# Two of eight convolved channel blocks of a hybrid SSD and conformer layer: their tap products are added by accumulating DMAs instead of by GpSimd

## The chip, the cores and the metric

The kernel runs on one core of a Trainium2 chip. The metric is the device time of that core in microseconds (us). The core's engines have their own instruction queues and wait for each other by semaphores: TensorE (PE in the profile, with PEld for its weight loads), VectorE (DVE), ScalarE (ACT), GpSimd (POOL) and SyncE (SP, which here only issues DMAs). Each queue is worked off in its order: an instruction that waits holds up all that stand behind it.

## The reference, cut to what matters

One layer, 1024 tokens by 1024 channels, all in float32. What is normalized by the first LayerNorm goes through one input projection, whose columns feed an SSD group (Mamba-2, with a convolution of 4 taps) and a conformer group; both meet in an output projection, followed by two more norms and a gate. The conformer group is where the change lies:

```
glu = glu + b_glu[i]
u = glu[..., :D_CONF] * jax.nn.sigmoid(glu[..., D_CONF:])
u = causal_depthwise_conv(u, conf_conv_w[i], conf_conv_b[i])   # 31 taps, 1024 channels
u = jax.nn.silu(layer_norm(u, conf_ln_g[i], conf_ln_b[i]))
y_conf = u * jax.nn.silu(cgate)
```

The convolution is depthwise: each channel's output is a sum of 31 shifted copies of its row, each times one weight. The LayerNorm after it needs all 1024 channels of a token.

## The kernel before, in words

Channels lie on the 128 partitions and the 1024 tokens along the free dimension. The input projection (`inproj`, L188) is made in 44 column tiles of 128 columns. For each, `weights` (L182) has SP load `wraw` (512 KB), ScalarE round it into `wh` and GpSimd take the rest into `wl` (`split`, L117 to L120). TensorE then multiplies for two halves of 512 tokens, for 8 blocks of the contracted dimension, three products each (L123 to L125): 48 matmuls of 128x512 for a column tile. ScalarE takes each half out of PSUM; three banks (`bank`, L77) hold the halves. The tiles `wraw`, `wh` and `wl` rotate through 8 buffers, so `wl` is made ahead of TensorE by two column tiles at most.

The conformer's 1024 channels are 8 blocks. `conf_tile(j)` (L254) makes two column tiles of the projection, then the gated product `u` with 30 columns of padding in front, then the convolution. For six blocks VectorE does all 31 taps into a PSUM tile `pc` (L291). For blocks 1 and 5 (`POOL_CONV`, L36), ScalarE makes the first tap into `acc` (L282) and then, for each of 30 taps, a product `prod` (L285), which GpSimd adds to `acc` (L286). `prod` has two buffers (tag `xd`): the product after next can start when an addition has read its own. Of the sums `acc`, `cs` adds up all eight on GpSimd (L628, L630), and `conf_norm` (L387) needs `cs` complete. Between the conformer's blocks the program places the column tiles of the SSD group: `xbc_tile` (its 4 taps on VectorE, L377) and `z_tile`.

The order of each engine's queue is set when the program is built, by a scheduler that runs the program against estimated durations; it interleaves the products, the casts and the evacuations on ScalarE, and the additions and the `wl` subtractions on GpSimd. After the projection come the normalization, chunks of the SSD scan and the output projections, which the change does not touch.

Of the kernel before, what the change touches and what calls it, by code (L numbers as in the profile page):

```python
# [11 lines left out]
ALU = mybir.AluOpType  # L12
PSUM = bass.MemoryType.PSUM

P = 128
# [10 lines left out]

# columns of the per-channel vectors
VEC = {}
# [18 lines left out]
def tile_block(ctx: ExitStack, tc: tile.TileContext, x, pT, wple, win, wdt, wout, wgate, vec, rows, heads, out):  # L47
# [17 lines left out]

# [1 line left out]
    BUFS = {"gt": 4, "xd": 2, "u": 2, "ha": 3, "y": 2, "xb": 2, "st": 1}  # L67
# [19 lines left out]

# [1 line left out]
    vc = const.tile([P, NVEC], F32, name="vc")  # L89
# [13 lines left out]
    nc.gpsimd.memset(mhalf, -0.5)  # L103
    # [s, l]: 1 where l >= s
    tri = const.tile([P, P], F32, name="tri")
    nc.gpsimd.affine_select(out=tri, in_=ones, pattern=[[1, P]], compare_op=ALU.is_ge, fill=0.0, base=0, channel_multiplier=-1)
    # adds rows h, 16 + h and 32 + h
    fold = const.tile([P, HEADS], F32, name="fold")
# [8 lines left out]
    def split(src, h, l, leng):  # L117
        """h: src rounded to the tensor engine's 12 bits; l: what is left, exactly."""
        nc.scalar.copy(out=h.bitcast(F32R), in_=src)  # L119
        leng.tensor_tensor(out=l.bitcast(F32R), in0=src, in1=h, op=ALU.subtract)  # L120
# [16 lines left out]
    def moments(src, tag):  # L137
        """mean and rstd of the rows of src [P, 1024]."""
        st = wk.tile([P, 2, 6], F32, name="st" + tag, tag="st" + tag)
        for i in range(2):  # L140
            nc.vector.bn_stats(out=st[:, i, :], in_=src[:, i * 512:(i + 1) * 512])
        mv = small("mv" + tag, 2)
        nc.vector.bn_aggr(out=mv, in_=st)
        return mv[:, 0:1], rstd_of(mv[:, 1:2], 1, tag, nc.gpsimd)
# [6 lines left out]

# [1 line left out]
    xts = [regB.tile([P, D], F32, name="xt", tag="B1") for t in range(NT)]  # L153
# [26 lines left out]

# [1 line left out]
    def weights(ct):  # L182
# [17 lines left out]
    def residual():  # L200
        ag, abb, bob = (work(n, "ha") for n in ("ag", "abb", "bob"))
        for i, tl in enumerate((ag, abb, bob)):
            nc.sync.dma_start(out=tl, in_=rows[i:i + 1, :].broadcast_to([P, D]))
        nc.gpsimd.tensor_scalar(out=ag, in0=ag, scalar1=ALPHA, scalar2=0.0, op0=ALU.mult, op1=ALU.add)
        nc.gpsimd.tensor_scalar(out=abb, in0=abb, scalar1=ALPHA, scalar2=0.0, op0=ALU.mult, op1=ALU.add)
        nc.gpsimd.tensor_tensor(out=abb, in0=abb, in1=bob, op=ALU.add)
        # alpha * h + b_out, by tokens
        for t in range(NT):
            nc.gpsimd.tensor_tensor(out=xts[t], in0=xts[t], in1=ag, op=ALU.mult)
            nc.gpsimd.tensor_tensor(out=xts[t], in0=xts[t], in1=abb, op=ALU.add)  # L210
            nc.sync.dma_start(out=ha_d[t], in_=xts[t])

    def ple_all():
        """the projected per-layer input, by tokens."""
        parts = {}
        tags = iter(["u", "u", "xd", "xd", "gt", "gt", "ha", "ha"])
        for src, nm in ((wple, "wp"), (pT, "pp")):
            for k in range(2):
                raw = work(nm + "raw", "xb") if nm == "wp" else regB.tile([P, L], F32, name=nm + "raw", tag="B2")
                parts[nm, k] = (raw, work(nm + "H", next(tags)), work(nm + "L", next(tags)))  # L220
        for half in range(2):
            hs = slice(half * 512, half * 512 + 512)
            for k in range(2):
                for src, nm in ((wple, "wp"), (pT, "pp")):
                    nc.sync.dma_start(out=parts[nm, k][0][:, hs], in_=src[:, k, hs])
                    split(*(a[:, hs] for a in parts[nm, k]), nc.vector)
        embed_load(0)
        nc.sync.dma_start(out=vc, in_=vec)
        nc.vector.tensor_scalar(out=hb, in0=v("bglu", 0, 16), scalar1=0.5, scalar2=None, op0=ALU.mult)
        parts = {i: (a[1].bitcast(F32R), a[2].bitcast(F32R)) for i, a in parts.items()}  # L230
        for t in range(NT):
            tk = slice(t * P, (t + 1) * P)
            pl = work("pl", "xb" if t % 4 > 1 else "y", L)
            for n in range(2):
                nn = slice(n * 512, n * 512 + 512)
                ps = bank("psp")
                for k in range(2):
                    three(ps, parts["pp", k][0][:, tk], parts["pp", k][1][:, tk], parts["wp", k][0][:, nn], parts["wp", k][1][:, nn], k == 0, k == 1)
                if (t + n) % 2:
                    nc.vector.tensor_copy(out=pl[:, nn], in_=ps)  # L240
                else:
                    nc.scalar.copy(out=pl[:, nn], in_=ps)
            nc.sync.dma_start(out=ple_d[t], in_=pl)
# [10 lines left out]
    def conf_tile(j):  # L254
        """GLU and the causal convolution of 128 channels."""
        ga = work("ga", "gt")
# [24 lines left out]
        if j in POOL_CONV:  # L281
            nc.scalar.activation(out=acc, in_=u[:, 0:L], func=AF.Identity, scale=v("ccw", j * KC), bias=v("ccb", j))  # L282
            for i in range(1, KC):
                pr = work("prod", "xd")
                nc.scalar.activation(out=pr, in_=u[:, i:i + L], func=AF.Copy, scale=v("ccw", j * KC + i))  # L285
                nc.gpsimd.tensor_tensor(out=acc, in0=acc, in1=pr, op=ALU.add)  # L286
        else:
            pc = pair("pc")
            first_tap(FT31, pc, u[:, 0:L], v("ccw", j * KC), v("ccb", j))
            for i in range(1, KC):  # L290
                nc.vector.scalar_tensor_tensor(out=pc if i + 1 < KC else acc, in0=u[:, i:i + L], scalar=v("ccw", j * KC + i), in1=pc, op0=ALU.mult, op1=ALU.add)  # L291
# [9 lines left out]
    def dt_path():  # L301
# [7 lines left out]
        nc.sync.dma_start(out=hd, in_=heads.unsqueeze(0).broadcast_to([P, 2, HEADS]))  # L309
        # both parts of the weights side by side  # L310
        nc.scalar.copy(out=wh2[:, :, 0:HEADS].bitcast(F32R), in_=raw)
# [22 lines left out]

        # softplus(v) = max(v, 0) + 2 atanh(e / (2 + e)), e = exp(-|v|)
        nc.vector.tensor_tensor(out=b3(vv), in0=b3(pst[:, 0:P]), in1=bh(hd[:, 0, :]), op=ALU.add)
# [16 lines left out]
    def decays():  # L353
        """dec holds dt * a at first: its sums over the tokens of each chunk, and what follows from them."""
        ar, er = (wk.tile([P, P], F32, name=n, tag="dg") for n in ("ar", "er"))
# [60 lines left out]
    def out_weight(src, get, tag, last, scale=None, leng=nc.gpsimd):  # L416
        """last: a place for the raw one, where those that share the tag leave none."""
        raw = work("wor", last) if last else get("wor", tag)
# [8 lines left out]

# [1 line left out]
    state = work("state", "st")  # L429
# [8 lines left out]
    def prep(c):  # L438
        """what chunk c needs besides the state: decays times C.B, x * dt, B by tokens."""
        xb = slabs(work("xb", "xb", 12 * P), 12)  # L440
# [8 lines left out]
        for q in range(2):  # L449
            er = ea_d[c * HEADS:(c + 1) * HEADS, :].rearrange("(t q) l -> q t l", q=2)[q]  # L450
            nc.sync.dma_start(out=ea[q * HD:(q + 1) * HD], in_=er.unsqueeze(0).broadcast_to([HD, NK, P]))
        # exp(acs[l] - acs[s]); the part l < s is held at exp(0) here and dropped with C.B
        for h in range(HEADS):
# [30 lines left out]
    def chunk(c, sz, xb, gg, ea, xdt, xdd, btok):  # L484
        y = slabs(work("y", "y"))
        for g in range(2):
            # from the state, scaled by exp(acs[l])
            ys = y[:, g * 4:g * 4 + 4, :]
# [34 lines left out]
    def mean_square(c, y, ea):  # L523
        """rstd of the two groups of channels of the gated output."""
        sq = ea.rearrange("p (g t) l -> p g t l", g=2)
# [21 lines left out]
    def conf_out(c, mH, mL, ha):  # L547
        """conformer half of the output projection"""
        for n in range(2):
# [14 lines left out]
    def affine(o, src, mu, rs, g, b):  # L564
        """(src - mu) * rs * g + b"""
        nc.vector.scalar_tensor_tensor(out=o, in0=src, scalar=mu, in1=g, op0=ALU.subtract, op1=ALU.mult)
        nc.vector.scalar_tensor_tensor(out=o, in0=o, scalar=rs, in1=b, op0=ALU.mult, op1=ALU.add)

    def out_proj(c, yH, yL):
        """the SSM half of the output projection, and the norm"""  # L570
        r = work("r", "ha")
# [21 lines left out]
    def gate(c, r, hTH, hTL):  # L593
        """the per-layer input, gated, and the norm"""
        pl = work("pl3", "st")
# [75 lines left out]

# [1 line left out]
    ready, last = out_proj(0, *ys.pop(0)), None  # L673
# [58 lines left out]
```

## Time and profile before

| | |
|---|---|
| runs of the kernel | 928.87 and 934.99 us, median 931.93 |
| profiled execution, span from the first to the last instruction | 927.1 us |
| the lower of the two runs less that span | 1.8 us |
| busy: PE, DVE, POOL, ACT | 877.1, 708.6, 534.4, 364.8 us |
| busy share of POOL from 150 to 250 us and from 350 to 450 us | 0.94 to 0.98 |
| the 60 additions into `acc` on GpSimd | 160.2 us |

An engine's busy time counts its compute instructions; matmuls overlap, so that the busy time of PE is no measure of how fast it works, while the distance between the starts of two matmuls is. Where an engine stands idle, the profile names what released it. The share of busy time is of the whole span; the change lies in two stretches of it.

### The profile page before, as it was taken

The numbers are of one execution on the slowest core, as the hardware profiler recorded it, in microseconds if no ns is written. First come the engines' busy times: TensorE is split into PE (matmuls) and PEld (weight loads), VectorE is DVE, ScalarE is ACT, GpSimd is POOL, SyncE is SP. The second block draws the span as 40 slices with busy tenths as digits, with TensorE's granted clock in tenths as the row PEclk, the third lists the DMA queues.
The fourth block names the chain that finished last, engine by engine and source line by source line (L and its number), as shares of the span: only waits on it lengthen the run. The fifth ranks groups of instructions, "written<-read, shape, count | busy, mean of one in ns | idle before, by whom it ended". The sixth has DMA issues, their size and how long they took to land.

```text
span 927.1 us, 10959 instructions
## 1 busy us (share of the span) xinstructions
PE 877.1 (95%) x4141; PEld 711.0 (77%) x4141; DVE 708.6 (76%) x830; ACT 364.8 (39%) x513; POOL 534.4 (58%) x298
## 2 busy tenths in 40 slices
PE   6989998989999999999899999999999889999996
PEld 5857787868787888788688887777777668888885
DVE  7868997498999989989626523998885786666665
ACT  3532244665423435555446533644343421111001
POOL 2559836999924249999792254676757442222211
PEclk9999999989999999999999999999999999999999
DMA  9703241321213121322322388888887902222111
GB/s 337 264 24 107 77 157 46 96 69 46 78 37 113 52 86 53 123 97 80 114 100 83 103 304 271 300 273 230 283 264 261 353 25 92 91 90 91 69 46 68
DMA packets 67716, 126.42 MB, mean 136 GB/s; under 512 B 4176, under 2 KB 41552, under 8 KB 67664
## 3 DMA queue, kind: packets, MB, share of 16 engines
q1 hardware_dynamic: 67664, 125.73, 40.4%
q8 instruction: 32, 0.52, 0.2%
q14 instruction: 20, 0.16, 0.1%
HBM read 89.93 MB, written 35.78 MB: 136 GB/s over the span
## 4 chain that ended last, share of the span: by engine, by line
PE 47%; DVE 20%; POOL 13%; DMA 11%; issue 6%; ACT 3%; SPq 1%; POOLq 0%; DVEq 0%; ACTq 0%
POOL acc L286 8%; DVE pc L291 7%; PE ps L123 6%; PE ps L124 6%; PE ps L125 6%; DVE cacc L377 4%; PE psg L123 3%; PE psg L125 3%; PE psg L124 3%; DMA wor<-in_wout_dram 3%; PE pss L123 3%; PE pss L125 3%; PE pss L124 3%; DMA xb<-xbc_d 2%; POOL wl L120 2%
## 5 line engine op out<-in xcount | busy, mean ns | idle before, releaser
L123 PE MATMUL ps<-hH,wl 128*128 128x512 f32 x704 | 278.4, 397 | 12.7 <-ACT ga L262 6.2
L124 PE MATMUL ps<-hL,wh 128*128 128x512 f32 x704 | 278.0, 395 | 1.0 <-DVE hL L179 1.0
L125 PE MATMUL ps<-hH,wh 128*128 128x512 f32 x704 | 278.1, 395 | 0.0
L291 DVE SCALAR_TENSOR_TENSOR pc<-u,vc,pc 128x1024 f32<-128x1024 f32 x174 | 223.8, 1286 | 4.5
L123 PEld LDWEIGHTS ps<-hH,wl 128*128 128x128 f32 x704 | 133.9, 191 | 44.7 <-issue 7.7
L286 POOL TENSOR_TENSOR acc<-acc,prod 128x1024 f32<-128x1024 f32 x60 | 160.2, 2671 | 13.3 <-ACT acc L282 9.3
L124 PEld LDWEIGHTS ps<-hL,wh 128*128 128x128 f32 x704 | 134.2, 191 | 29.3 <-DVE hL L179 1.5
L125 PEld LDWEIGHTS ps<-hH,wh 128*128 128x128 f32 x704 | 134.2, 191 | 28.4 <-issue 0.2
L120 POOL TENSOR_TENSOR wl<-wraw,wh 128x1024 fp32r<-128x1024 f32 x44 | 110.6, 2513 | 53.2 <-ACT wh L119 23.0
L132 POOL TENSOR_SCALAR ve<-mv 128x1 f32<-128x1 f32 x24 | 21.7, 907 | 121.3 <-DVE mv L611 88.4
L285 ACT ACTIVATE prod<-u,vc 128x1024 f32<-128x1024 f32 x60 | 68.8, 1150 | 51.4 <-POOL acc L286 44.9
L377 DVE SCALAR_TENSOR_TENSOR cacc<-xin,vc,cacc 128x1024 f32<-128x1024 f32 x36 | 76.9, 2135 | 7.4 <-ACT cacc L247 4.7
L119 ACT CAST wh<-wraw 128x1024 fp32r<-128x1024 f32 x44 | 46.2, 1051 | 82.6 <-DMA wraw<-in_win_dram 47.8
L455 DVE TENSOR_SCALAR gt<-gt,acs 128x128 f32<-128x128 f32 x128 | 42.0, 397 | 25.4 <-POOL qs L398 17.3
L123 PE MATMUL psg<-woh,hTL 128*128 128x512 f32 (+1 forms) x136 | 52.9, 389 | 4.8 <-DVE hTL L120 4.8
L123 PE MATMUL pso<-woh,mL 128*128 128x512 f32 x128 | 51.6, 406 | 2.8 <-POOL mL L120 1.8
L123 PE MATMUL pss<-woh,yL 128*128 128x512 f32 x128 | 50.8, 397 | 3.4 <-DVE r L580 3.4
L120 POOL TENSOR_TENSOR wol<-wor,woh 128x1024 fp32r<-128x1024 f32 x12 | 32.7, 2743 | 36.1 <-ACT woh L119 36.1
L125 PE MATMUL pso<-woh,mH 128*128 128x512 f32 x128 | 53.2, 417 | 0.0
L125 PE MATMUL psg<-woh,hTH 128*128 128x512 f32 (+1 forms) x136 | 52.6, 387 | 0.0
L124 PE MATMUL psg<-wol,hTH 128*128 128x512 f32 (+1 forms) x136 | 52.1, 383 | 0.0
L124 PE MATMUL pso<-wol,mH 128*128 128x512 f32 x128 | 50.9, 397 | 0.0
(184 smaller groups left out, 1435.5 us busy)
## 6 DMA issues: line engine op xcount, KB each, us to landing
wraw<-in_win_dram SPq DMA_DIRECT2D x44, 512.0 KB, 4.1
gt<-acs_d SPq DMA_DIRECT2D x16, 512.0 KB, 4.6
wor<-in_wout_dram SPq DMA_DIRECT2D x16, 512.0 KB, 6.1
xbc_d<-cacc SPq DMA_DIRECT2D x12, 512.0 KB, 3.4
xb<-xbc_d SPq DMA_DIRECT2D x8, 768.0 KB, 6.3
xt<-in_x_dram SPq DMA_DIRECT2D x8, 512.0 KB, 9.2
ple_d<-pl SPq DMA_DIRECT2D x8, 512.0 KB, 5.0
ha_d<-xt SPq DMA_DIRECT2D x8, 512.0 KB, 5.2
```

The source lines that it names most:

```text
L119: nc.scalar.copy(out=h.bitcast(F32R), in_=src)
L120: leng.tensor_tensor(out=l.bitcast(F32R), in0=src, in1=h, op=ALU.subtract)
L123: mm(ps, lhsT=ll, rhs=rh, start=first, stop=False)
L124: mm(ps, lhsT=lh, rhs=rl, start=False, stop=False)
L125: mm(ps, lhsT=lh, rhs=rh, start=False, stop=last)
L132: eng.tensor_scalar(out=ve, in0=var, scalar1=EPS, scalar2=None, op0=ALU.add)
L285: nc.scalar.activation(out=pr, in_=u[:, i:i + L], func=AF.Copy, scale=v("ccw", j * KC + i))
L286: nc.gpsimd.tensor_tensor(out=acc, in0=acc, in1=pr, op=ALU.add)
L291: nc.vector.scalar_tensor_tensor(out=pc if i + 1 < KC else acc, in0=u[:, i:i + L], scalar=v("ccw", j * KC + i), in1=pc, op0=ALU.mult, op1= ...
L377: nc.vector.scalar_tensor_tensor(out=acc, in0=xin[:, j:j + L], scalar=v("scw", i * 4 + j), in1=acc, op0=ALU.mult, op1=ALU.add)
L455: nc.vector.tensor_scalar(out=sl, in0=sl, scalar1=col(acs, c, h), scalar2=0.0, op0=ALU.subtract, op1=ALU.min)
```

## The change

The addition of each product to `acc` in blocks 1 and 5 is no longer an instruction of GpSimd's own datapath. GpSimd's queue issues a DMA from `prod` to `acc` (both in SBUF, 128 rows of 4 KB), which adds to what it finds in `acc`. All else in the text of the program stays (the rest of the diff deletes comments, line by line):

```
@@ -283,7 +283,7 @@
             for i in range(1, KC):
                 pr = work("prod", "xd")
                 nc.scalar.activation(out=pr, in_=u[:, i:i + L], func=AF.Copy, scale=v("ccw", j * KC + i))
-                nc.gpsimd.tensor_tensor(out=acc, in0=acc, in1=pr, op=ALU.add)
+                nc.gpsimd.dma_start(out=acc, in_=pr, accum_op=ALU.add)
         else:
             pc = pair("pc")
             first_tap(FT31, pc, u[:, 0:L], v("ccw", j * KC), v("ccb", j))
```

The scheduler orders the queues anew. GpSimd's queue within block 1, before (`x3` stands for three in a row; a name in brackets is a semaphore that is waited for: `DMAHW` of a DMA that SP issued, `DMASW` of one that GpSimd issued, the others of an engine):

```order
L120 TENSOR_TENSOR wl<-wraw,wh 128x1024 [waits DMAHW2_49,PE_49]
L286 TENSOR_TENSOR acc<-acc,prod 128x1024 [waits Activation_49,Pool_49] x3
L120 TENSOR_TENSOR wl<-wraw,wh 128x1024 [waits DMAHW4_49,PE_49]
L286 TENSOR_TENSOR acc<-acc,prod 128x1024 [waits Activation_49,Pool_49] x4
L120 TENSOR_TENSOR wl<-wraw,wh 128x1024 [waits DMAHW5_49,PE_49]
L286 TENSOR_TENSOR acc<-acc,prod 128x1024 [waits Activation_49,Pool_49] x3
```

The same place in the queue after the change:

```order
L120 TENSOR_TENSOR wl<-wraw,wh 128x1024 [waits DMAHW4_49,PE_49,Pool_49]
L286 DMA acc<-prod 128x1024 [waits DMASW7_49,Activation_49]
L286 DMA acc<-prod 128x1024 [waits DMASW0_49,Activation_49]
L286 DMA acc<-prod 128x1024 [waits DMASW1_49,Activation_49]
L120 TENSOR_TENSOR wl<-wraw,wh 128x1024 [waits DMAHW5_49,PE_49,Pool_49]
L286 DMA acc<-prod 128x1024 [waits DMASW2_49,Activation_49]
L286 DMA acc<-prod 128x1024 [waits DMASW3_49,Activation_49]
```

The pattern of about three additions to one `wl` stays, and each DMA waits for the semaphore of the DMA before it. From the first to the last DMA of block 1 GpSimd's queue now holds 10 `wl` subtractions (8 between the first and the last addition before), and in block 5 it holds 11 (9 before).

ScalarE's queue in block 1, before, around two casts of weights (`wh`) and the evacuations `ga` and `tb` of the conformer's next column tiles:

```order
L285 ACTIVATE prod<-u,vc 128x1024 [waits Pool_49]
L119 CAST wh<-wraw 128x1024 [waits DMAHW0_49,Pool_49]
L262 ACTIVATE ga<-ps_1487,hb 128x512 [waits PE_49]
L285 ACTIVATE prod<-u,vc 128x1024 [waits Pool_49] x2
L378 ACT_TABLE_LOAD
L378 ACTIVATE cacc<-cacc 128x1024 [waits DVE_49]
L285 ACTIVATE prod<-u,vc 128x1024 [waits Pool_49]
L262 ACTIVATE ga<-ps_1513,hb 128x512 [waits PE_49]
L119 CAST wh<-wraw 128x1024 [waits DMAHW2_49,Pool_49]
```

And after:

```order
L285 ACTIVATE prod<-u,vc 128x1024 [waits DMASW2_49]
L119 CAST wh<-wraw 128x1024 [waits DMAHW0_49,Pool_49]
L285 ACTIVATE prod<-u,vc 128x1024 [waits DMASW3_49]
L262 ACTIVATE ga<-ps_1487,hb 128x512 [waits PE_49]
L378 ACT_TABLE_LOAD
L378 ACTIVATE cacc<-cacc 128x1024 [waits DVE_49]
L285 ACTIVATE prod<-u,vc 128x1024 [waits DMASW4_49,Activation_49]
L262 ACTIVATE ga<-ps_1513,hb 128x512 [waits PE_49]
L285 ACTIVATE prod<-u,vc 128x1024 [waits DMASW5_49,Activation_49]
L119 CAST wh<-wraw 128x1024 [waits DMAHW2_49,Pool_49]
```

The products stand among the casts and evacuations as before, four between and around these two casts; each now waits for the landing of the DMA that read its buffer, where it waited for GpSimd.

## Rows read from the trace of the kernel before

**Rows 1.** Windows from first to last addition of blocks 1 and 5; columns in its heading.

```profile
core 0: us, PE busy (x) PEld busy (x) DVE busy (x) ACT busy (x) POOL busy (x), PEclk, DMA share, GB/s
136.07:248.93 112.86, 105.95 (x449) 86.22 (x448) 91.00 (x61) 61.09 (x67) 101.74 (x46) 0.95 0.20 62
340.67:445.02 104.35, 103.98 (x462) 85.68 (x461) 97.30 (x71) 55.57 (x61) 102.78 (x42) 1.00 0.27 83
```

**Rows 2.** Timeline of POOL in block 1: start, duration (us), line, tiles, count.

```profile
163.41 2.41 POOL L120 TENSOR_TENSOR wl<-wraw,wh 128x1024 fp32r<-128x1024 f32 x1
165.77 7.37 POOL L286 TENSOR_TENSOR acc<-acc,prod 128x1024 f32<-128x1024 f32 x3
173.09 2.41 POOL L120 TENSOR_TENSOR wl<-wraw,wh 128x1024 fp32r<-128x1024 f32 x1
```

**Rows 3.** Timeline of PE at the granted clock 1.0; nine starts, the first and the last.

```profile
222.96 0.39 PE L123 MATMUL ps<-hH,wl 128*128 128x512 f32 x1
...
224.77 0.39 PE L125 MATMUL ps<-hH,wh 128*128 128x512 f32 x1
```

**Rows 4.** Waits in block 1: engine, line waited for, us in total, times, longest.

```profile
ACT prod L285 <- POOL acc L286: 20.1, 17, 2.2
...
PE ps L123 <- ACT ga L262: 3.5, 1, 3.5
PE ps L123 <- ACT xin L373: 3.4, 2, 2.6
```

**Rows 5.** Timeline of ACT in block 1: in brackets the idle time before, its releaser.

```profile
192.04 1.16 ACT L285 ACTIVATE prod<-u,vc 128x1024 f32<-128x1024 f32 x1 [1.70 <-POOL acc L286]
195.38 1.15 ACT L285 ACTIVATE prod<-u,vc 128x1024 f32<-128x1024 f32 x1 [2.19 <-POOL acc L286]
196.55 1.28 ACT L378 ACT_TABLE_LOAD   x1
197.85 1.06 ACT L378 ACTIVATE cacc<-cacc 128x1024 f32<-128x1024 f32 x1
198.81 1.13 ACT L285 ACTIVATE prod<-u,vc 128x1024 f32<-128x1024 f32 x1
199.85 0.67 ACT L262 ACTIVATE ga<-ps,hb 128x512 f32<-128x512 f32 x1
```

**Rows 6.** Timeline of PE behind that `ga`, at the granted clock 0.5 after a wait.

```profile
196.80 0.39 PE L125 MATMUL ps<-hH,wh 128*128 128x512 f32 x1
200.66 0.76 PE L123 MATMUL ps<-hH,wl 128*128 128x512 f32 x1 [3.47 <-ACT ga L262]
201.22 0.63 PE L124 MATMUL ps<-hL,wh 128*128 128x512 f32 x1
...
202.93 0.63 PE L125 MATMUL ps<-hH,wh 128*128 128x512 f32 x1
...
205.91 0.42 PE L123 MATMUL ps<-hH,wl 128*128 128x512 f32 x1
```

**Rows 7.** DMA issues: tensors, queue, count, size, median us from issue to landing.

```profile
wraw<-in_win_dram SPq DMA_DIRECT2D x44, 512.0 KB, 4.1
...
xbc_d<-cacc SPq DMA_DIRECT2D x12, 512.0 KB, 3.4
...
out_dram<-gt SPq DMA_DIRECT2D x7, 512.0 KB, 2.6
```

**Rows 8.** DMA queue of SP: packets, MB, time as share of 16 engines' span.

```profile
q1 hardware_dynamic: 67664, 125.73, 40.4%
```

**Rows 9.** Instructions of line 286 and of the tile `cacc`: minimum, median, maximum in ns.

```profile
L286 POOL TENSOR_TENSOR acc<-acc,prod x60: 2348/2412/3391, 136.1 to 442.6; 128x1024 f32<-128x1024 f32 x60
L377 DVE SCALAR_TENSOR_TENSOR cacc<-xin,vc,cacc x36: 1276/2222/3473, 95.8 to 376.3; 128x1024 f32<-128x1024 f32 x36
```

More of the change, by code (lines that the diff above doesn't have):

```diff
@@ L285, in conf_tile @@
                 nc.scalar.activation(out=pr, in_=u[:, i:i + L], func=AF.Copy, scale=v("ccw", j * KC + i))
-                nc.gpsimd.tensor_tensor(out=acc, in0=acc, in1=pr, op=ALU.add)
+                nc.gpsimd.dma_start(out=acc, in_=pr, accum_op=ALU.add)
         else:
```

## The prediction

> **What bounds the kernel now.** I first asked, in the windows, how busy each engine is between the first and the last addition of each of the two blocks. Together the stretches last 112.86 + 104.35 = 217.2 us, and GpSimd is busy for 204.5 us of that [rows 1]. So GpSimd, which the whole span shows at little over half its time, is full just where the change is made. Then the timeline of GpSimd there: one `wl` of 2.4 us and three additions of 7.4 us take 173.09 - 163.41 = 9.7 us [rows 2], and that is one column tile of the projection. Then TensorE's pace, from the starts of its matmuls: 8 steps in 224.77 - 222.96 = 1.81 us, 0.226 us each [rows 3], so 48 matmuls are 10.9 us. GpSimd and TensorE thus keep step within a tenth. The two stretches hold 449 + 462 = 911 matmuls [rows 1], 19.0 column tiles or 206 us at that pace; only 217.2 - 206 = 11 us are lost to waits and to the lower clock.
>
> The waits show how GpSimd's lateness reaches TensorE: not by `wl` first, but through ScalarE. ScalarE's `prod` waited for GpSimd 17 times in block 1, and TensorE waited 3.5 and 3.4 us for ScalarE's evacuations [rows 4]. One such case can be followed: two products wait 1.70 and 2.19 us for additions, the evacuation `ga` stands behind them in ScalarE's queue and comes at 199.85, and TensorE, out of PSUM banks since 196.80, goes on at 200.66 after 3.47 us [rows 5, 6].
>
> **The change, part by part.** It removes 60 additions of 2.35 to 3.39 us from GpSimd [rows 9]. In their place stand 60 DMAs on the same queue, each of which waits for the landing of the one before, since it adds to the same `acc`. So what counts is one link of a chain, L, from the issue of one DMA to the issue of the next. Thirty links in a row take 30 L, and GpSimd's queue cannot pass them: behind a waiting DMA stand the `wl` subtractions, the memsets of `u` and `xin`, and the sums `cs`. TensorE waits for `wl`; SP's next `wraw` and ScalarE's next `wh` wait for the buffers that TensorE then holds longer. ScalarE waits too: its product after next needs the landing, and behind that product stand casts and evacuations. What is gained is that a `wl` now runs while a DMA is under way, so its 2.4 us cost nothing as long as L is longer than that.
>
> The new order has 10 and 11 `wl` inside the two chains, so 60 links are spread over 21 column tiles. At the pace of before these take 217.2 x 21 / 19.0 = 240 us. TensorE has some work in hand when a chain starts: three banks of half a tile each and `wl` at most two tiles ahead. I count one tile, 11 us, for each chain, 22 us in all. The added time is therefore 60 L - 240 - 22. It is zero at L = 4.4 us.
>
> *The price of L.* No DMA issued by GpSimd and none that adds is in the trace, so I bound it by copies of 512 KB. From below: the stores of `out`, the same 128 rows of 4 KB from SBUF, land after 2.6 us, and nothing is charged for the addition [rows 7]. An adding DMA has to read the old `acc` as well. SP's queue moved 125.73 MB in 40.4% of 16 engines' 927.1 us [rows 8], so 336 GB/s with all 16 at work, and a second read of 512 KB is 1.6 us. From above: two passes as slow as the median load of `wraw`, 2 x 4.1 = 8.2 us [rows 7]. I take the median load and one more read, 4.1 + 1.6 = 5.7 us. The load is the right neighbour because it runs in these stretches beside the same traffic; the store of `cacc`, also from there, takes 3.4 us [rows 7] and would give 5.0. What GpSimd needs to write a DMA's descriptors has no row, and is a reason not to go below 5.
>
> With L = 5.7: 60 x 5.7 = 342, and 342 - 240 - 22 = **80 us more**. A column tile then takes three links, 17 us, instead of 11.
>
> What else moves is free. ScalarE's 60 products stay the same. VectorE's steps on `cacc` run from 1.28 to 3.47 us, median 2.22 [rows 9]; they may get faster with GpSimd's adds gone, at most 36 x (2.22 - 1.28) = 34 us on an engine that TensorE does not wait for in rows 4. The added DMA traffic, 60 times 1.6 to 3.2 us of all engines, meets queues that are busy 0.20 to 0.27 of the time there [rows 1]. After block 5 `cs` ends later by what the chain is late, and so does TensorE; I charge nothing twice.
>
> The profiled execution has a span of 927.1 us, and the lower run lies 1.8 us above it: 928.9 + 80 = 1009. From the median of the two runs, 931.9, it is 1012. I predict **1010 us**.
>
> **The rivals.** *The chain stays under TensorE's pace (not slower).* One mechanism: the DMA's second read overlaps its first, or the store of 2.6 us is the better neighbour. With 2.6 + 1.6 = 4.2 us, 60 links are 252 us, under the 262 that TensorE's work and its lead cover; it decides below 4.4 us for no loss and below 4.7 us for a loss under 2%. The gain is capped by the 11 us which TensorE lost in the two stretches: 918 to 930 us. For it speaks the store of 2.6 us; against it that even the copies in these very stretches take 3.4 and 4.1 us before a second read is paid. Chance 0.20. The Trainium skill (DMA: Bandwidth & Descriptors, "Anatomy of one DMA — SWDGE (gpsimd) path") speaks for this rival: it fits a GpSimd-issued DMA by about 2.0 us plus the bytes at 436 GB/s, which for 512 KB gives an estimate of 3.2 us. The same skill (Collectives: The Full Stack, "The bandwidth ceiling: the fold count and why AG ≠ RS ≠ AR") says that an adding DMA costs two source reads; with both in the fit the estimate is 4.4 us, just at the break. By that rule the time would be 930, by the rows 1010; no run shown here has such a DMA.
>
> *Two passes.* The read of `acc`, the addition and the write follow each other without overlap, or GpSimd is slow to issue: L = 8.2 us, 492 - 262 = +230 us, **1159 us**. For it: each link is a full round trip with nothing to overlap, and loads under more traffic do take longer than 4.1. Against: 16 engines work on rows of their own and can overlap. Chance for L above 7.0 us: 0.22.
>
> *The clock goes with it.* TensorE would stand idle for 17.1 - 10.9 = 6.2 us of each column tile. After the wait of 3.47 us it ran at the granted clock 0.5, 1.2 of 2.4 GHz: 201.22 to 202.93 is 4 steps of 0.43 us, until 205.91 [rows 6]. If it stayed at that level all through the chains, a column tile would take 48 x 0.43 = 20.5 us, more than three links: 21 x 20.5 = 430, and 430 - 262 = +168 us, **1097 us**. Against: it went back to full speed after some 5 us, and as long as three links are the slower, a slow TensorE costs nothing. Chance 0.08.
>
> **How the numbers follow.** The forecast, L between 4.7 and 7.0 us, has the remaining chance of 0.50, and its own range is 929 + 20 to 929 + 158, or 949 to 1087 us. The range for 8 in 10 reaches from the first rival's times to the second's price: 925 to 1160. Outside lie the last of the gains and links over 8.2 us. A measurement of this kernel can tell about 2%, 18.6 us, from no change. Faster by more than that: 0.02, as only 11 us are to be had. Within 2%: 0.18. Slower: 0.50 + 0.22 + 0.08 = 0.80.
>
> **What would show it.** Sixty DMAs `acc<-prod` with a median from issue to landing near 5.7 us, and starts of theirs on GpSimd as far apart. The two chains should last about 171 us each instead of 113 and 104. TensorE's idle time there should be put down to ScalarE's evacuations and to `wl`, and ScalarE's `prod` should wait for a DMA, not for GpSimd. Before the first chain, between the chains and after the second, the stages should last as before. The prediction is wrong if the links are under 4.4 us, if TensorE keeps its pace although they are longer (a lead that I did not see), or if time is lost outside the chains.

## The result and the profile after

The changed kernel takes 1032.86 us (two runs, 1029.81 to 1035.91) against 931.93: a ratio of 1.107, 95% interval 1.102 to 1.113. The forecast was 1010 with a range of 925 to 1160. Direction and main mechanism were right, and the size fell short: 80 us were forecast, 101 came. The profiled execution has a span of 1028.1 us, 101.0 more than before.

The windows of the two chains, from the issue of the first DMA to the landing of the last (the engine that comes next, GpSimd with its sum `cs`, starts there):

```profile
core 0: us, PE busy (x) PEld busy (x) DVE busy (x) ACT busy (x) POOL busy (x), PEclk, DMA share, GB/s
136.39:309.70 173.31, 139.26 (x538) 109.65 (x537) 99.72 (x78) 67.58 (x75) 51.17 (x48) 0.90 0.64 140
379.76:548.57 168.81, 144.98 (x605) 117.44 (x603) 95.20 (x73) 62.74 (x82) 54.91 (x44) 0.93 0.73 165
```

Against [rows 1] they last 342.1 us instead of 217.2, and GpSimd is busy for less than a third of that instead of nearly all. An engine that was full is now mostly idle, and the stretch is longer. 342.1 us for 60 links is 5.70 us a link, the value of the forecast. The timeline of GpSimd shows what it does instead (start, duration, line; in brackets the idle time before, and what ended it):

```profile
221.16 0.88 POOL L286 DMA_DIRECT2D acc<-prod  x1 [4.35 <-DMA acc<-prod]
226.22 0.86 POOL L286 DMA_DIRECT2D acc<-prod  x1 [4.19 <-DMA acc<-prod]
231.31 0.86 POOL L286 DMA_DIRECT2D acc<-prod  x1 [4.23 <-DMA acc<-prod]
231.88 2.69 POOL L120 TENSOR_TENSOR wl<-wraw,wh 128x1024 fp32r<-128x1024 f32 x1
236.94 0.88 POOL L286 DMA_DIRECT2D acc<-prod  x1 [2.37 <-DMA acc<-prod]
```

Issues stand 5.1 us apart (226.22 to 231.31); the `wl` at 231.88 runs under a DMA's way, as the shorter idle time behind it shows, and its link is 5.6 us, half a us longer. Over all links it costs little: the kernel below that takes `wl` off GpSimd has the same median link, 5.2 us. The additions of [rows 2] stood 2.4 us apart. The waits in the first chain:

```profile
POOL acc L286 <- DMA acc<-prod: 96.8, 25, 6.6
ACT prod L285 <- DMA acc<-prod: 84.2, 27, 8.0
...
PE ps L123 <- ACT tb L265: 15.1, 6, 4.9
...
PE ps L123 <- ACT xin L373: 12.0, 4, 4.3
```

As in [rows 4], TensorE waits for ScalarE's evacuations, only longer, and ScalarE's product now waits for a landing. The timeline of ScalarE shows the evacuation `tb` among products that wait:

```profile
220.70 1.15 ACT L285 ACTIVATE prod<-u,vc 128x1024 f32<-128x1024 f32 x1 [5.91 <-DMA acc<-prod]
221.76 1.03 ACT L119 CAST wh<-wraw 128x1024 fp32r<-128x1024 f32 x1
222.70 0.68 ACT L265 ACTIVATE tb<-ps,hb 128x512 f32<-128x512 f32 x1
225.76 1.16 ACT L285 ACTIVATE prod<-u,vc 128x1024 f32<-128x1024 f32 x1 [2.39 <-DMA acc<-prod]
230.86 1.15 ACT L285 ACTIVATE prod<-u,vc 128x1024 f32<-128x1024 f32 x1 [3.94 <-DMA acc<-prod]
231.92 0.67 ACT L265 ACTIVATE tb<-ps,hb 128x512 f32<-128x512 f32 x1
```

The two halves of one column tile (`tb` at 222.70 and 231.92) are taken out 9.2 us apart, where TensorE needs 5.4 us for a half. The page's DMA issues and queues, to set beside [rows 7, 8], give the new operation's price (q1 is SP's queue, q0 is GpSimd's):

```profile
q1 hardware_dynamic: 67664, 125.73, 36.5%
q0 software_dynamic: 8640, 31.46, 16.2%
...
acc<-prod POOLq DMA_DIRECT2D x60, 512.0 KB, 4.6
wraw<-in_win_dram SPq DMA_DIRECT2D x44, 512.0 KB, 4.7
...
xbc_d<-cacc SPq DMA_DIRECT2D x12, 512.0 KB, 4.5
```

**Where the time went.** I take the start of each column tile, that is of every 48th of the 2,112 matmuls of the projection, in each trace, less the same in the kernel before. This is how late TensorE is, in us, for the changed kernel and those of the experiments:

```
column tile         8   14   18   20   28   34   36   37   38   41   42   last matmul
changed            -2   23   40   46   45   69   73   83   81   84   97   97
block 1 alone      -2   23   41   41   41   38   41   41   41   41   41   41
block 5 alone       0    0    0    0    2   31   34   45   43   46   60   60
no end             -4   21   37   44   43   71   72   85   85   84   84   84
copies             -1   -2   -1   -1   -2   -6   -9   -7   -9   -6    7    7
half the columns   -4   15   20   19   18   31   40   40   42   42   42   42
traffic            -1    0    2    1    0    0    3    3    3    3    3    3
two sums           -2   21   22   21   26   50   47   49   49   48   48   48
wl on VectorE      -2   26   40   39   41   65   68   86   84   87  101  101
blocks 1, 4 DMA     2   28   46   45   86   90   91   91   95   96   96   96
blocks 1, 4 POOL    0    0    2    2   10    5    5    5    5   12   12   12
four buffers        1   24   27   26   25   21   20   20   20   20   20   20
mixed               2   20   19   18   17   13   13   13   13   13   13   13
```

In the changed kernel TensorE is 40 us late at the end of the first chain (tiles 7 to 18) and 46 at tile 20. The rest of the stretch between the chains adds nothing, the second chain (tiles 24 to 36) another 27, and then, behind the second chain, 24 more come. The output projections behind add 4. So up to the end of the second chain 73 us are lost, near the forecast of 80, and most of the rest is a loss behind the chain, which the forecast had at nothing.

### The profile page after: what moved, and what is told of

The parts are those of the page before. It is cut to its first block, busy times and chain, and to the rows that moved or that the text cites. A ratio compares the mean times of both kernels' runs of the same rounds, so it can differ in the third digit from the quotient of the medians.

```text
span 1028.1 us, 11009 instructions
## 1 busy us (share of the span) xinstructions
PE 906.8 (88%) x4141; PEld 727.9 (71%) x4141; DVE 688.9 (67%) x830; ACT 365.3 (36%) x513; POOL 428.4 (42%) x298
## 3 DMA queue, kind: packets, MB, share of 16 engines
q0 software_dynamic: 8640, 31.46, 16.2%
## 5 line engine op out<-in xcount | busy, mean ns | idle before, releaser
L123 PE MATMUL ps<-hH,wl 128*128 128x512 f32 x704 | 289.1, 412 | 77.8 <-ACT zt L383 18.3
L124 PE MATMUL ps<-hL,wh 128*128 128x512 f32 x704 | 285.7, 406 | 0.7 <-DVE hL L179 0.7
L125 PE MATMUL ps<-hH,wh 128*128 128x512 f32 x704 | 285.6, 406 | 0.0
L123 PEld LDWEIGHTS ps<-hH,wl 128*128 128x128 f32 x704 | 139.3, 198 | 116.7 <-issue 43.5
L125 PEld LDWEIGHTS ps<-hH,wh 128*128 128x128 f32 x704 | 139.1, 198 | 30.9 <-issue 0.5
L124 PEld LDWEIGHTS ps<-hL,wh 128*128 128x128 f32 x704 | 139.3, 198 | 30.0 <-DVE hL L179 1.1
L286 POOL DMA_DIRECT2D acc<-prod x60 | 52.2, 870 | 225.2 <-DMA acc<-prod 204.4
L120 POOL TENSOR_TENSOR wl<-wraw,wh 128x1024 fp32r<-128x1024 f32 x44 | 113.5, 2579 | 51.8 <-PE ps L123 24.1
L377 DVE SCALAR_TENSOR_TENSOR cacc<-xin,vc,cacc 128x1024 f32<-128x1024 f32 x36 | 56.3, 1563 | 30.6 <-ACT cacc L247 30.5
```

What stands on the lines that cost most here:

```text
L123: mm(ps, lhsT=ll, rhs=rh, start=first, stop=False)
L124: mm(ps, lhsT=lh, rhs=rl, start=False, stop=False)
L125: mm(ps, lhsT=lh, rhs=rh, start=False, stop=last)
L286: nc.gpsimd.dma_start(out=acc, in_=pr, accum_op=ALU.add)
L377: nc.vector.scalar_tensor_tensor(out=acc, in0=xin[:, j:j + L], scalar=v("scw", i * 4 + j), in1=acc, op0=ALU.mult, op1=ALU.add)
```

## The experiments

Theory: a serial chain of 60 landings, which reaches TensorE through ScalarE, and whose second end delays the normalization. Rivals: the traffic of the DMAs, the price of the addition alone, GpSimd's blocked `wl`, the clock, the new order.

**Each chain alone.** Edit of the first (the second has `j == 5`):

```
+                if j == 1:
+                    nc.gpsimd.dma_start(out=acc, in_=pr, accum_op=ALU.add)
+                else:
+                    nc.gpsimd.tensor_tensor(out=acc, in0=acc, in1=pr, op=ALU.add)
```

> Only block 1's products are added by DMAs; block 5's by GpSimd as before. Theory (the serial chain): the 30 links again take some 173 us, TensorE is 46 us late at the end of the first chain as in the changed kernel, and nothing is given back or added behind it: 929 + 46 = 975 us. Rival (a large part of the loss comes from the order or the DMA traffic as such, wherever the DMAs are): the loss is half of the whole 101, or 980 us with the lateness growing after the chain too, above all behind block 5.

Measured: 973.0 us, ratio 1.042 (1.034 to 1.051). TensorE is 41 us late behind the chain and stays so to the end: the theory, 2 us off, and no loss behind this chain.

> Only block 5's products are added by DMAs. Theory (behind block 5 stands the normalization, which needs all eight sums, so that the end of that chain sets the end of the projection): the chain takes 169 us instead of 104, all of the difference but some 6 us is lost, 929 + 58 = 987 us, of which about 25 us come after the chain's end. Rival (as the prediction counted it: a lead of TensorE is kept): 169 - 11 column tiles of 11.4 us - 11 us = 32 us, 961 us.

Measured: 994.7 us, ratio 1.066 (1.058 to 1.074). The loss is 34 us at tile 36 and 60 at the end, so 26 us come behind the chain. The theory is 8 us too low, and the prediction's own bookkeeping, which ended at 961, is refuted. The two kernels' losses, about 40 and 61 us over the 933.3 us that the kernel before took beside them, add up to the whole 101.

**Nobody waits for the end of the second chain.** Edit:

```
-        elif j > 1:
+        elif j > 1 and j != 5:
             nc.gpsimd.tensor_tensor(out=cs, in0=cs, in1=accs[j], op=ALU.add)
```

and the loops over the eight sums in `conf_norm` leave out k = 5.

> As the changed kernel, but nobody waits for the end of block 5's chain: that block's sum is left out of the mean and the variance and is not normalized (12 VectorE, GpSimd and ScalarE instructions fewer). Theory (the normalization behind the chain is where the last 24 us were lost): TensorE is 73 us late at the chain's end and stays so, 929 + 75 = 1004 us. Rival (the last 24 us come from the clock, from the DMA traffic or from the new order): 1025 to 1033 us.

Measured: 1017.1 us, ratio 1.090 (1.081 to 1.098), between both; the kernel has 7 instructions fewer, not 12. Half of the loss behind the chain is gone (24 falls to 12). The table shows which half. In the changed kernel TensorE loses 10 us between tiles 36 and 37, where it waits for `cs`, and 13 or 14 between tiles 41 and 42, where it waits for the evacuation `cg`. Here the second loss is gone, and the first is not. TensorE's waits from 505 to 660 us:

```profile
PE mu L390 <- POOL cs L630: 10.9, 1, 10.9
PE rb L409 <- DVE dg L408: 7.3, 1, 7.3
PE ps L123 <- ACT cg L296: 3.1, 1, 3.1
```

The wait of 10.9 us for the sums `cs` of the other blocks, which still stand among the DMAs in GpSimd's queue, lies inside the chain and is made up by tile 36. Behind the chain TensorE waits for `dg`, which needs the variance. GpSimd's timeline shows that the variance is late too, since the additions of the squares (`qs`) stand among the last DMAs and end at 555.1:

```profile
536.68 5.18 POOL L398 TENSOR_TENSOR qs<-qs,sq 128x1024 f32<-128x1024 f32 x2
542.22 0.88 POOL L286 DMA_DIRECT2D acc<-prod  x1 [0.36 <-DMA acc<-prod]
547.51 7.56 POOL L398 TENSOR_TENSOR qs<-qs,sq 128x1024 f32<-128x1024 f32 x3
```

The wait for the block's sum was taken away, but not the queue in which the rest of the normalization stands. VectorE then takes the variance up at 566.7 only, after work of the scan that stands before it; which of the two delays counts is not shown. So this run supports the theory by half and does not settle it; the next pair goes further.

**The second chain earlier.** Edit to the changed kernel and to the kernel before: `POOL_CONV = (1, 4)`.

> As the changed kernel, but the second block whose products are added by DMAs is block 4 instead of 5, so that VectorE's blocks 5 to 7 follow the second chain and its end is not the last thing the normalization waits for. To be read against the next kernel, which has the same blocks with GpSimd's additions. Theory (the last 24 to 26 us are lost because the end of the second chain starts the normalization): only what the two chains cost by themselves, 65 to 80 us over the next kernel. Rival (that loss comes with a second chain wherever it lies: clock, traffic, order): 95 us or more over it.

> The kernel before, with block 4 instead of 5 for ScalarE and GpSimd: the base for the kernel above. Both theories: near the kernel before, 925 to 950 us.

Measured: 1021.9 us with DMAs, ratio 1.097 (1.089 to 1.104), and 943.6 with GpSimd's additions, 1.013 (1.008 to 1.018); the difference of the medians, 78 us, is what the theory said. The two runs with DMAs lie 12 us apart, and the profiled one, the slower, is 86 us over its base. The path is a little different: the lateness over the base is 76 us at tile 28 and 85 at tile 30 (95 against 10), and then does not grow: 84 at the last matmul. So nothing is lost behind the chains, but the chains cost more than 73 in this execution. The second one has only 10 `wl` between its first and last DMA, where the changed kernel has 11, and one column tile less under the same 30 links is 11 us more.

**What a link is made of.** First, the DMAs copy and do not add (`accum_op` is left out).

> As the changed kernel, but the 60 DMAs only copy: each overwrites the sum, nothing is added. Same bytes written, same waits. Theory A (an adding DMA pays for a second read, 1.6 us of the 5.1 us from link to link in quiet stretches): links of about 3.5 us, 60 of them 210 to 240 us, under TensorE's 240 plus its lead: 925 to 945 us. Theory B (the round trip from GpSimd's issue to its next one is the price, the addition is nearly free): links of 4.7 us or more, 1000 us and over.

Measured: 947.5 us, ratio 1.015 (1.006 to 1.024). Line 286 in this kernel, its landings, and GpSimd's timeline:

```profile
L286 POOL DMA_DIRECT2D acc<-prod x60: 530/530/767, 136.5 to 456.3; - x60
...
DMA to landing us min/median/max: 2.8/3.0/7.3
```

```profile
206.58 0.53 POOL L286 DMA_DIRECT2D acc<-prod  x1 [6.38 <-DMA acc<-prod]
209.96 0.53 POOL L286 DMA_DIRECT2D acc<-prod  x1 [2.85 <-DMA acc<-prod]
```

The median distance of two issues in a chain is 3.5 us, against 5.2 in the changed kernel (5.1 where it is quiet). So the addition costs 1.6 us a link, as much as the second read that the prediction worked out from the queue's bytes; GpSimd's queue is also busy 0.33 us longer per DMA, and no run separates the two. The loss goes from 101 us to 16. Theory A holds; the time is 2 us over its range.

The rest of the loss says more. TensorE is 9 us early at tile 38 and 7 us late at the end. The second chain ends later than before, at 459.47 instead of 445.02 [rows 1], and TensorE then waits for `cg`, which it does not in the kernel before (GpSimd's timeline, and TensorE's waits from 460 to 585 us):

```profile
459.47 2.40 POOL L630 TENSOR_TENSOR cs<-cs,acc 128x1024 f32<-128x1024 f32 x1 [2.66 <-DMA acc<-prod]
PE ps L123 <- ACT cg L296: 10.5, 1, 10.5
```

So the loss behind the second chain comes even where TensorE keeps its pace through both chains. Another 9 us come behind the projection; they are not explained.

Second, the DMAs add 512 of the 1024 columns (`out=acc[:, 0:512], in_=pr[:, 0:512]`).

> As the changed kernel, but each DMA adds only the first 512 of the 1024 columns (half of the sum is left out). It splits a link into a part for each DMA and a part for its bytes. If the DMA engines' time of 2.8 us per adding DMA is what scales, a link falls from 5.1 to about 3.7 us, and the time to 930 to 945 us. If a link is mostly a fixed round trip it stays near 5 us, and the time over 1010 us.

Measured: 975.8 us, ratio 1.050 (1.040 to 1.059), between both. A quiet link is 3.8 to 4.0 us and a landing 3.3: half of the bytes take 1.2 us off a link of 5.1, so, if the rest goes with the bytes, some 2.7 us do not depend on them. The time is higher than the range for such links, as the scheduler put only 8 and 9 `wl` into the chains instead of 10 and 11.

**Traffic without a chain.** Edit to the kernel before:

```
                 nc.gpsimd.tensor_tensor(out=acc, in0=acc, in1=pr, op=ALU.add)
+                nc.sync.dma_start(out=next(junk), in_=pr)
```

> The kernel before (GpSimd adds), with one store of each product to a place in HBM that nobody reads, issued by SP: 60 more DMAs of 512 KB in the same stretches, without a chain; a product's buffer is now held by its store too. Theory (the chain, not the traffic): the stores cost 0 to 10 us, 929 to 942 us. Rival (the DMAs crowd the loads of weights, which ScalarE then waits for): with 1.6 us of all engines per store against 2.8 of an adding DMA, over half of the 101 us, 985 us or more.

Measured: 934.8 us, ratio 1.0045 (1.0012 to 1.0078): 60 more DMAs of 512 KB in the same stretches cost 3 us (1 to 7 by the interval). Traffic of this size is not where the time goes. That an adding DMA keeps the DMA engines busy longer than such a store leaves room for some us.

**Which way the chain reaches TensorE.** VectorE makes `wl` of the column tiles in the chains:

```
+        n = len(made) - 1
-        split(raw, wh, wl, nc.gpsimd)
+        split(raw, wh, wl, nc.vector if 9 <= n <= 19 or 28 <= n <= 38 else nc.gpsimd)
```

> As the changed kernel, but for 22 column tiles (those whose weights are made while the chains run) VectorE makes wl instead of GpSimd. It asks by which way the chain reaches TensorE. If through the wl that stand behind waiting DMAs in GpSimd's queue: TensorE is freed of the first chain, 955 to 985 us. If through ScalarE, whose products wait for landings with casts and evacuations behind them: 1025 to 1040 us as in the changed kernel, and TensorE's waits are put down to ScalarE's evacuations.

Measured: 1034.1 us, ratio 1.113 (1.103 to 1.123), the changed kernel's time. With all but one `wl` of the chains off GpSimd's queue the loss is the same, and TensorE waits as before for ScalarE:

```profile
PE ps L123 <- ACT ga L266: 13.7, 4, 5.1
PE ps L123 <- ACT xin L377: 9.5, 5, 4.9
PE ps L123 <- ACT tb L269: 8.8, 4, 3.4
```

So the way is ScalarE: two product buffers tie its queue to the landings, and the evacuations stand in that queue.

**Two sums, two DMAs under way.** The odd taps go to `acc`, the even ones to a sum in HBM (`odd_d`, the name is the wrong way round), and a last DMA adds that one to `acc`.

> As the changed kernel, but the even taps go into a second sum, which lies in HBM, and one last DMA adds that one to acc: as many adding DMAs, but each waits for the one before the last, so that two are under way. Theory (the chain of landings): about half a link for a tap, 2.6 to 3.2 us, so 3 taps for a column tile fit under TensorE's 10.9 us and the loss is gone: 918 to 945 us. Rival (traffic, or what GpSimd and the DMA engines need for an adding DMA as such): 1000 us or more.

Measured: 980.3 us, ratio 1.055 (1.047 to 1.062). Both missed: half of the loss is gone, but a tap takes 3.7 us in the median. The timeline of GpSimd says that a DMA now waits for its product:

```profile
191.09 0.87 POOL L292 DMA_DIRECT2D odd_d<-prod  x1 [3.34 <-ACT prod L286]
193.57 0.87 POOL L288 DMA_DIRECT2D acc<-prod  x1 [1.61 <-ACT prod L286]
```

A landing of 5.4 to 5.7 us, and then a product of 1.15 us in the buffer that it freed, make the turn of each buffer, as long as there are two. With four of them, and block 5 as before:

```
-                pr = work("prod", "xd")
+                pr = work("prod", "y" if j == 1 and (i - 1) % 4 > 1 else "xd")
```

> Block 5 as before (GpSimd adds). Block 1 with two sums, one of them in HBM, as in the earlier kernel with two sums, but with four product buffers instead of two. Theory (with two sums the two product buffers hold the chain: a product can start only when the DMA before the last has landed, and its own DMA after it): with four buffers a tap takes about 2.8 to 3.2 us, and the loss of the first chain, 41 us with one sum and 20 us with two, falls under 10 us: 925 to 942 us. Rival (two adding DMAs under way slow each other or GpSimd's issue so far that nothing is won): 3.7 us or more for a tap and 950 us or more.

Measured: 951.4 us, ratio 1.019 (1.014 to 1.025); TensorE is 20 us late at the end, no better than the first chain with two buffers (21). The steady part of the chain is what the theory said: the issues of one sum are 5.8 us apart, a tap 2.9 us.

```profile
188.04 0.89 POOL L294 DMA_DIRECT2D odd_d<-prod  x1 [0.33 <-issue]
190.26 0.87 POOL L290 DMA_DIRECT2D acc<-prod  x1 [1.33 <-DMA acc<-prod]
193.84 0.87 POOL L294 DMA_DIRECT2D odd_d<-prod  x1 [2.71 <-DMA odd_d<-prod]
196.03 0.87 POOL L290 DMA_DIRECT2D acc<-prod  x1 [1.31 <-DMA acc<-prod]
199.63 0.87 POOL L294 DMA_DIRECT2D odd_d<-prod  x1 [2.73 <-DMA odd_d<-prod]
```

But over the chain, the last DMA from `odd_d` included, a tap takes 3.8 us, since single links are longer, and this order has 7 `wl` in it. TensorE's work for 7 column tiles is 80 us at the pace of before, and the chain takes 120. The expectation failed on that, not on the buffers.

**A mixture.** In block 1 GpSimd adds the odd taps and DMAs the even ones; four buffers.

```
-                nc.gpsimd.dma_start(out=acc, in_=pr, accum_op=ALU.add)
+                if j != 1 or i % 2:
+                    nc.gpsimd.tensor_tensor(out=acc, in0=acc, in1=pr, op=ALU.add)
+                elif i == 2:
+                    nc.gpsimd.dma_start(out=odd_d, in_=pr)
+                else:
+                    nc.gpsimd.dma_start(out=odd_d, in_=pr, accum_op=ALU.add)
```

> Block 5 as before. In block 1 GpSimd adds the odd taps to acc and DMAs add the even taps to a sum in HBM, which a last DMA adds to acc; four product buffers. A candidate to beat both kernels: no addition waits for a landing less than two taps old, and GpSimd, which is full in block 1 of the kernel before, issues 15 DMAs of 0.86 us instead of 15 additions of 2.4 to 3.4 us. Theory: TensorE's 11 us of loss in block 1 go, 920 to 928 us against 931. Rival (GpSimd's queue still stops at a landing now and then): 931 to 945 us.

Measured: 942.3 us, ratio 1.011 (1.008 to 1.014): 1% slower than before, the rival. GpSimd's queue still stops at landings, and its additions stand behind them:

```profile
189.36 0.88 POOL L292 DMA_DIRECT2D odd_d<-prod  x1 [2.44 <-ACT er L375]
189.98 2.68 POOL L288 TENSOR_TENSOR acc<-acc,prod 128x1024 f32<-128x1024 f32 x1
199.56 0.87 POOL L292 DMA_DIRECT2D odd_d<-prod  x1 [6.91 <-DMA odd_d<-prod]
200.17 2.65 POOL L288 TENSOR_TENSOR acc<-acc,prod 128x1024 f32<-128x1024 f32 x1
```

No version with adding DMAs beat the kernel before.

## Why the prediction was right, and where it fell short

*What bounds.* Right. GpSimd was full in the two stretches, and TensorE hung on ScalarE's evacuations behind products. The kernel with `wl` on VectorE shows that this way is enough to carry the loss; the prediction had named `wl` beside it, which did not matter.

*The price of a link.* 5.7 us was measured, 5.70 on the mean, but the sum of 4.1 + 1.6 is right by two errors that cancel. The addition costs 1.6 us, as worked out. The base is 3.5 us, the copy's link, not the 4.1 of a load of weights; that makes 5.1, near the median of the links, 5.2. The mean is half a us above that because 19 of the 58 links within the chains are longer than 5.6 us. That these two differences cancel is luck, and what makes single links long is open. The longest, the first with 10.3 us, is no landing: GpSimd's queue waited for VectorE before the memsets of `u` and `xin`, and the second DMA stood behind them. In 13 of the 19 SP issued a DMA within the link or in the 3 us before it, but so it did in 23 of the 39 shorter ones. The estimates that the prediction worked out from the Trainium skill (DMA: Bandwidth & Descriptors, "Anatomy of one DMA — SWDGE (gpsimd) path"), 3.2 us for a copy and 4.4 us with both reads, agree within 0.2 us with the landings, 3.0 and 4.6 us; a link also holds some 0.5 us between a landing and the next issue, and single links are longer, so that the chain came out on the slow side of the break.

*The lateness in the chains.* 80 us forecast, 73 measured, of which 7 came just behind the first chain (tiles 18 to 19), where TensorE waited 4.7 us for the evacuation `xin`; with block 1 alone that step is missing. TensorE's lead was somewhat larger than one column tile: by its matmuls it passed 11.1 tiles during the first chain and 12.3 during the second, where the order holds 10 and 11 `wl`.

*What failed.* The sentence "After block 5 `cs` ends later by what the chain is late, and so does TensorE; I charge nothing twice." The prediction had named "time is lost outside the chains" as a sign that it is wrong, and 24 of the 101 us were. The sentence is wrong since TensorE was credited with a lead in the same sum. A lead means that at the chain's end TensorE has done more of the projection than before, so that less of it is left to cover the normalization, which only starts there. The windows from the end of the second chain to the end of the projection show it, before and after:

```profile
445.02:567.70 122.68, 120.14 (x539) 98.35 (x539) 49.99 (x86) 59.04 (x78) 60.66 (x25) 0.99 0.45 148
```

```profile
548.57:665.00 116.43, 97.39 (x422) 78.52 (x424) 45.14 (x83) 51.83 (x58) 54.94 (x23) 0.93 0.39 131
```

TensorE has 117 matmuls less to do there, 26 us at 0.226 us, and needs only 6 us less. The stretch is set by the normalization, from `cs` to the normalized sums. In the timeline its two ends in TensorE's queue are a wait for `cs` and one for the gate's evacuation behind the normalized sums:

```profile
558.03 3.61 PE L390 MATMUL mu<-cs,invd 128*128 128x512 f32 x4 [6.59 <-POOL cs L630]
...
635.41 0.80 PE L123 MATMUL ps<-hH,wl 128*128 128x512 f32 x1 [10.47 <-ACT cg L296]
```

So the lead of the second chain had no worth, and what the first had saved was given back too: the end of the last chain came 548.57 - 445.02 = 103.6 us later, and the projection's end 97 us. That the loss is zero behind block 1 alone, 26 us behind block 5 alone and zero again with the second chain earlier shows the place. So does the copying kernel, which loses time nowhere else in the projection. TensorE's lateness grows by 10 us at the first of the two waits and by 13 or 14 at the second. Which step of the normalization sets each is not settled, as the kernel without the second end removed only half.

One tie to the chain's end was named nowhere: the scan's `xdt` (L462) takes a buffer of the tag `xd`, the two that `prod` has. VectorE stood still for it for 45.8 us, until a product was read by its DMA just before the chain's end. Nothing shows that this held TensorE up in this kernel, since VectorE then waited again, for `mu`:

```profile
543.47 1.23 DVE L462 TENSOR_TENSOR xdt<-xtok,dtok 128x1024 f32<-128x1024 f32 x1 [45.77 <-DMA acc<-prod]
560.15 9.66 DVE L392 TENSOR_TENSOR acc<-acc,mu 128x512 f32<-128x512 f32 x16 [15.46 <-PE mu L390]
```

*The rivals.* The first (not slower) needed links under 4.4 us. The copying kernel, with a mean of 4.3 and 4.0 us within its chains, bears that break out for the chains alone: TensorE is not late at tile 36. For the time it does not hold, since 16 us are lost even so. Two passes were not needed. The granted clock fell from 0.95 and 1.00 to 0.90 and 0.93 in the chains, where TensorE often stood idle. By the starts of its matmuls, steps between 0.3 and 0.6 us took 24 us beyond the full pace in the two chains, and 5 us before the change. How much of that lies on the path was not tested; links, order and lead give the chains' cost without it.

*What else moved.* VectorE's steps on `cacc` fell to the bottom of their range, as the prediction allowed, and no wait of TensorE in the first chain names them:

```profile
L377 DVE SCALAR_TENSOR_TENSOR cacc<-xin,vc,cacc x36: 1271/1282/3430, 95.8 to 414.7; 128x1024 f32<-128x1024 f32 x36
```

Their median was 2222 ns [rows 9]. The Trainium skill (SBUF — State Buffer, "Who interferes with whom") says that a VectorE instruction with two SBUF inputs contends with GpSimd's reads; the trace agrees, the median step being 0.94 us shorter with the additions gone.

## What to carry to other kernels

An accumulation moved from an engine to DMAs becomes a chain of landings: price it as links, one round trip each, and not by the engine time that it frees. Compare the links with the bounding engine's work that the queue's order places beside them, and count that order anew, as the scheduler deals it out by its own idea of the DMA's length. A lead that hides the start of a delay is worth nothing where the delayed thing itself starts a long dependent stretch.

## What the runs showed of the hardware

- An adding DMA of 512 KB from SBUF to SBUF lands after 4.6 us in the median (4.5 at least), a copy of the same shape from the same queue after 3.0. GpSimd's queue is busy for 0.86 us per adding DMA and 0.53 per copy; half of the bytes do not change the 0.86.
- Two adding DMAs under way, one to SBUF and one to HBM, land after 5.3 to 5.7 us instead of 4.6 in the median, and give one tap in 2.9 us in the steady part instead of 5.1: more than one at a time pays, but by less than two.
- The adding DMAs took 16.2% of 16 engines' span for 31.46 MB written, 2.8 us of all engines each; the copies 8.4%, 1.3 us each.
